# The first layer's memory values as seven half-size products, woven with two query heads

## The chip, the cores and the metric

The kernel runs on one core of a Trainium2 chip. The metric is device time in microseconds (us) of one execution, from the program's start to its end. TensorE (PE) multiplies matrices into PSUM banks of 128 partitions by 512 numbers; VectorE (DVE), ScalarE (ACT) and GpSimd (POOL) work on SBUF and PSUM; SyncE (SP) issues most transfers. Each engine runs its own instructions in order and waits on semaphores for those of others.

## The reference, cut to what matters

Two layers (512 positions, width 1024): each a mixer, a cross-attention into 256 memory rows and a SwiGLU feed-forward, all with a norm before and a norm after. The first layer's mixer is forgetting attention (FoX) beside a short gated convolution. All numbers are 32-bit floats.

```python
for layer in range(DEPTH):
    h = rmsnorm(x, g_mix_pre[layer])
    y = fox_shortconv_mixer(h, ...) if layer % 2 == 0 else rglru_mixer(h, ...)
    x = x + rmsnorm(y, g_mix_post[layer])
    h = rmsnorm(x, g_cross_pre[layer])
    m = rmsnorm(mem, g_mem[layer])
    y = memory_cross_attention(h, m, w_xq[layer], w_xkv[layer], w_xo[layer])
    x = x + rmsnorm(y, g_cross_post[layer])
    ...

def memory_cross_attention(h, m, w_q, w_kv, w_o):
    q = (h @ w_q).reshape(bsz, seq, MEM_HEADS, MEM_HEAD_DIM)
    k, v = jnp.split(m @ w_kv, 2, axis=-1)
    ...
```

The change concerns v of the first layer, a product of 256 x 1024 by 1024 x 1024, and the two first heads of q (512 x 1024 by 1024 x 256 each).

## The kernel before, in words

**Products.** A product of floats is made as three on TensorE: each operand is split into a rounded part hi and a rest lo, and hi·hi, hi·lo and lo·hi are added in one bank. `split_out` (L553-562) makes the two: a CAST on ScalarE (L556) and a subtraction on VectorE (L557). Weights come in pieces of 128 x 1024 numbers (512 KB) on SP's queue into one of four raw tiles `st`, and are split into one of four pairs `wh`, `wl` (`load_w`, L111-137).

**Stages around the change.** FoX ends with the output projection's second half (`half1`, L617-637). There each of four blocks of 128 positions of x is finished (`chain`, L638-650): the sum of squares on ScalarE (L221), a factor by small operations on VectorE (L225, L229) and a power on POOL (L233), x updated from two halves ya and yb (L642, L645). Then follow the next norm, two more sums of squares, a factor and the product h (L259). TensorE transposes h (L306) into a bank, and ScalarE and VectorE bring it out as hTh and hTl (`put_T`, L315 and L316). The blocks t = 0 and 1 are transposed between the matmuls of `half1`, t = 2 and 3 at the end of the keys. Between them the memory rows are transposed (L1034), copied out as `mTr` (L1037), stored to DRAM for the second layer as memT (L1050, POOL) and scaled by the gain g_mem and split into `mT` (L1043 ScalarE, L1044 VectorE).

**Keys, values, heads.** `memory_kv` (L1057-1093) computes the keys in four chunks of 256 columns with the banks of pool A (L1071, L1072; taken out by L1074, L1075 and split into kh, kl), then the transposes of blocks 2 and 3 into banks of pool B (`between`), then the values in two halves of 512 columns, also in pool A: for each of two halves 8 row blocks of weights x 2 blocks of memory rows x 3 matmuls (L1088-1090), taken out by four splits. `cross` then runs the query heads (`q_head`, by `ws_gemm` and `mm3`, L336-339): the weights stand still as lhsT and hT moves.

**Order.** The order of TensorE is the order in which the program is written. The order on the other engines is set by the tile scheduler from its own estimates. Two lists give the DRAM-side sums of the feed-forward's down projection, which is already made of seven products: `copies` are DRAM-to-DRAM copies, which `pace` issues on SP after three of every four weight loads; `adds` are transfers that add to DRAM, which `spend` issues on POOL, at some places behind a one-column copy `at` (L151) that waits for a given tile. `weave` runs two generators of matmul steps, a step of the one and a step of the other in turn.

Of the kernel before, what the change touches and what calls it, by code (L numbers as in the profile page):

```python
# [8 lines left out]
F32 = mybir.dt.float32  # L9
# [17 lines left out]
HOOKS = 0, 2  # L27
G = 14
SB = 8
GB = 6  # L30
# [12 lines left out]
def trunk_kernel(ctx: ExitStack, tc: tile.TileContext, a: dict, out: bass.AP):  # L43
# [625 lines left out]
    class DownProj(OutProj):  # L669
# [56 lines left out]
        def put_y(self, jp):  # L726
            if jp in self.stg:
                pool[0] = nc.gpsimd.dma_start(out=self.y[:, jp // 2, :, jp % 2, :],
                                              in_=self.stg[jp].rearrange("p m h c -> p (m h) c")).ins
                if jp:  # L730
                    spend(1)

# [266 lines left out]


    memT = dram.tile([P, KT, MEM], F32, name="memT")

# [16 lines left out]
    def memory_T(layer, bank):  # L1019
# [33 lines left out]
        if layer:  # L1053
            return vhl, (lambda: parts(range(4)), lambda: parts(range(4, KT)))
        return vhl, (lambda: turn(0), last)

    def memory_kv(layer, vhl, between):  # L1057

        w = a["w_xkv"][layer]
        kh_, kl_ = group("kh"), group("kl")  # L1060
        kh = kh_.rearrange("p a (b c) -> p (a b) c", c=MEM)
        kl = kl_.rearrange("p a (b c) -> p (a b) c", c=MEM)
        for c in range(4):
# [30 lines left out]

    def cross(layer, hT, kv, proj, hTf):
        kh, kl, vh, vl = kv
# [3 lines left out]
        qs, ps_, pts = {}, {}, {}  # L1100

        def q_head(h):
            banks = ws_gemm(wq, h * 256, hT)
            q = group("q")
            for m in range(2):
                split_out(banks[m], q[:, m, :], q[:, 2 + m, :], scale)
            qs[h] = q
            spend(3, f(q)[:, 3, 511:512])

# [50 lines left out]

        q_head(0)
        q_head(1)
        scores(0)
# [79 lines left out]
    def fox(proj):  # L1243
# [132 lines left out]
        TO = [(0, 0), (1, 0), (2, 0), (1, 384)]  # L1376

        def y_group(m):
            if m not in yg:
# [5 lines left out]
        def qk_pairs(m0):  # L1385
# [94 lines left out]
        def conv(m0):  # L1480
# [144 lines left out]

    hT = prev = None
    for layer in range(2):
# [3 lines left out]
        pf.plan()  # L1631
        pm = OutProj(a["ab_w_out"][0] if layer == 0 else a["c_w_out"][0], None, KT,
                     a["g_mix_post"][layer], a["g_cross_pre"][layer], hTc, *((bankA, bankB) if layer == 0 else (bankB, bankA)))
# [3 lines left out]
        else:  # L1637
            rglru(hT, prev, pm)
        vhl, steps = memory_T(layer, pm.first)
        pm.half1(steps)  # L1640
# [6 lines left out]

        kv = memory_kv(layer, vhl, rest)
        hTf = new_quads()
        pc = OutProj(a["w_xo"][layer], None, KT, a["g_cross_post"][layer], a["g_ffn_pre"][layer], hTf)  # L1650
        cross(layer, hTc, kv, pc, hTf)
        hT = new_hT() if layer == 0 else None
# [27 lines left out]
```

## Time and profile before

| | us |
|---|---|
| median of three runs | 1379.41 |
| lowest, highest | 1379.23, 1379.92 |
| the profiled execution | 1379.94 |
| its span, first to last instruction | 1378.2 |
| TensorE busy in it | 1368.9 |
| VectorE busy | 1119.8 |
| ScalarE busy | 730.9 |

The profile is one execution. A line such as L1088 is a line of the kernel before; matmuls overlap, so the time of one matmul is the distance between starts. The keys of the first layer begin at 227.1 us of the span, the transposes behind them at 249.7, the values at 251.4 and the first query head at 273.2.

### The profile page before, as it was taken

Reading aid. Unit: us, or ns where it says so; the run is one execution under the profiler, and the core shown is the slowest. Engines: PE = TensorE matmul, PEld = TensorE weight load, DVE = VectorE, ACT = ScalarE, POOL = GpSimd, SP = SyncE. Lnnn points to the kernel's source line nnn. Section 1 sums busy time; section 2 is a strip of 40 time slices with the busy share of each in tenths; the row PEclk is TensorE's granted clock in tenths of the full one; section 3 lists DMA queues with packets and bytes.
Section 4 is the critical chain, followed back from the end, with each engine's and each line's share of the span. In section 5 each row is a group of like instructions: output and inputs, shape, how many; then the busy total and the mean of one; then the engine's idle time right before and its main releaser. Section 6 shows DMA issues by size and latency. Waiting matters only on the chain.

```text
span 1378.2 us, 21545 instructions
## 1 busy us (share of the span) xinstructions
PE 1368.9 (99%) x8262; PEld 1217.7 (88%) x8262; DVE 1119.8 (81%) x1850; ACT 730.9 (53%) x1206; POOL 111.2 (8%) x160
## 2 busy tenths in 40 slices
PE   9999999999999999999999999999999999999998
PEld 7888788888899999998889888888889999999886
DVE  6777778635589999989898898764568999999987
ACT  5345466534464444456684896553456444445664
POOL 1000001012000101000011000101200011000001
PEclk9999999999999999999999999999999999999999
DMA  6854353668125557566666657357712555666654
GB/s 222 287 174 162 109 194 88 206 154 169 62 92 167 150 148 187 161 246 217 201 221 189 217 170 246 84 185 156 155 61 93 169 155 171 157 176 237 201 190 144
DMA packets 155107, 233.34 MB, mean 169 GB/s; under 512 B 8462, under 2 KB 90482, under 8 KB 153724
## 3 DMA queue, kind: packets, MB, share of 16 engines
q1 hardware_dynamic: 134420, 179.73, 39.5%
q0 software_dynamic: 17072, 46.16, 15.2%
q10 hardware_dynamic: 3512, 6.08, 1.4%
q8 instruction: 65, 1.06, 0.3%
q14 instruction: 38, 0.31, 0.1%
HBM read 219.34 MB, written 58.74 MB: 202 GB/s over the span
## 4 chain that ended last, share of the span: by engine, by line
PE 99%; DVE 0%; DMA 0%; ACT 0%; issue 0%; DVEq 0%; SPq 0%; ACTq 0%
PE bA L337 13%; PE bA L339 13%; PE bA L338 13%; PE bB L337 6%; PE bB L338 6%; PE bB L339 6%; PE bB L822 3%; PE bB L823 3%; PE bB L821 3%; PE bA L1071 2%; PE bA L822 2%; PE bA L823 2%; PE bA L821 2%; PE bA L580 2%; PE bA L582 2%; PE bB L582 2%
## 5 line engine op out<-in xcount | busy, mean ns | idle before, releaser
L557 DVE TENSOR_TENSOR wl<-st,wh 128x1024 fp32r<-128x1024 f32 x108 | 131.2, 1220 | 83.9 <-ACT wh L556 83.3
L556 ACT CAST wh<-st 128x1024 fp32r<-128x1024 f32 x108 | 113.1, 1050 | 107.9 <-PE bA L338 55.1
L337 PE MATMUL bA<-hTh,wh 128*128 128x512 f32 (+1 forms) x440 | 168.6, 383 | 0.0
L339 PE MATMUL bA<-hTh,wl 128*128 128x512 f32 (+1 forms) x440 | 165.6, 376 | 0.0
L338 PE MATMUL bA<-hTl,wh 128*128 128x512 f32 (+1 forms) x440 | 165.5, 376 | 0.0
L448 ACT CAST wg<-wr 128x1024 fp32r<-128x1024 f32 x80 | 83.6, 1046 | 48.9 <-DVE wr L477 38.5
L787 ACT CAST wh<-st 128x1024 fp32r<-128x1024 f32 x76 | 74.9, 985 | 62.4 <-PE bA L823 27.0
L449 DVE TENSOR_TENSOR wg<-wr,wg 128x1024 fp32r<-128x1024 f32 x80 | 97.1, 1214 | 0.0
L337 PEld LDWEIGHTS bA<-hTh,wh 128*128 128x128 f32 x440 | 82.9, 188 | 15.3 <-issue 1.0
L339 PEld LDWEIGHTS bA<-hTh,wl 128*128 128x128 f32 x440 | 82.8, 188 | 15.3
L338 PEld LDWEIGHTS bA<-hTl,wh 128*128 128x128 f32 x440 | 83.0, 189 | 13.8
L792 DVE TENSOR_TENSOR wl<-st,wh 128x1024 fp32r<-128x1024 f32 x76 | 86.1, 1133 | 10.2 <-ACT wh L787 10.1
L448 ACT CAST wh<-tt 128x1024 fp32r<-128x1024 f32 x40 | 42.1, 1053 | 61.4 <-DVE tt L477 61.4
L337 PE MATMUL bA<-hTq,wh 128*128 128x256 f32 x208 | 59.2, 284 | 0.0
L339 PE MATMUL bA<-hTq,wl 128*128 128x256 f32 x208 | 58.9, 283 | 0.0
L338 PE MATMUL bA<-hTq,wh 128*128 128x256 f32 x208 | 58.8, 283 | 0.0
L821 PE MATMUL bB<-wh,ya 128*128 128x512 f32 x148 | 57.6, 389 | 0.0
L822 PE MATMUL bB<-wl,ya 128*128 128x512 f32 x148 | 57.6, 389 | 0.0
L823 PE MATMUL bB<-wh,ya 128*128 128x512 f32 x148 | 57.6, 389 | 0.0
L767 DVE TENSOR_TENSOR ya<-yb,ya 128x512 fp32r<-128x512 f32 x84 | 53.3, 638 | 0.0
L821 PE MATMUL bA<-wh,ya 128*128 128x512 f32 x132 | 51.3, 389 | 0.0
L822 PE MATMUL bA<-wl,ya 128*128 128x512 f32 x132 | 51.3, 389 | 0.0
(385 smaller groups left out, 4396.9 us busy)
## 6 DMA issues: line engine op xcount, KB each, us to landing
wr<-in_w_ffn_gu_dram SPq DMA_DIRECT2D x80, 512.0 KB
st<-t SPq DMA_DIRECT2D x40, 512.0 KB
t<-in_w_ffn_down_dram SPq DMA_DIRECT2D x32, 512.0 KB
st<-in_w_xkv_dram SPq DMA_DIRECT2D x32, 512.0 KB
st<-in_w_ffn_down_dram SPq DMA_DIRECT2D x30, 512.0 KB
st<-in_ab_w_in_dram SPq DMA_DIRECT2D x24, 512.0 KB
y<-yr POOLq DMA_DIRECT2D x18, 512.0 KB, 4.7
t<-in_w_ffn_down_dram POOLq DMA_DIRECT2D x16, 512.0 KB, 8.7
```

Of the source, the lines that this page charges most:

```text
L337: nc.tensor.matmul(out=ps, lhsT=wh, rhs=xh, start=first, stop=False)
L338: nc.tensor.matmul(out=ps, lhsT=wh, rhs=xl, start=False, stop=False)
L339: nc.tensor.matmul(out=ps, lhsT=wl, rhs=xh, start=False, stop=last)
L448: return (lambda: nc.scalar.copy(out=to[0], in_=src), lambda: nc.vector.tensor_tensor(out=to[1], in0=src, in1=f(to[0]), op=ALU.subtract))
L449: lambda: nc.vector.tensor_tensor(out=to[1], in0=src, in1=f(to[0]), op=ALU.subtract))
L556: nc.scalar.copy(out=hi, in_=src)
L557: nc.vector.tensor_tensor(out=lo, in0=src, in1=f(hi), op=ALU.subtract)
L787: nc.scalar.copy(out=self.wt[s][0], in_=self.st[s])
L792: nc.vector.tensor_tensor(out=lo, in0=self.st[s], in1=f(hi), op=ALU.subtract)
L821: nc.tensor.matmul(out=banks[t], lhsT=yh, rhs=wh[:, jj, :], start=first and jj == 0, stop=False)
L822: nc.tensor.matmul(out=banks[t], lhsT=yh, rhs=wl[:, jj, :], start=False, stop=False)
L823: nc.tensor.matmul(out=banks[t], lhsT=yl, rhs=wh[:, jj, :], start=False, stop=last and jj == n - 1)
```

## The change

The values of the first layer become seven products of half size by Winograd's form of Strassen's scheme. With the normed memory split into row halves and inner halves (a11 ... a22) and the weights into inner and column halves (b11 ... b22), the seven products are a11·b11, s2·t2, n3·t3, a22·t4, n1·t1, a12·b21, n4·b22, each of 128 x 512 by 512 x 512.

- The weight sums t1 ... t4 are made in DRAM: eight copies of 512 KB on SP, ahead of the down projection's twenty in the list, and eight adding transfers on POOL, each behind an `at` copy, issued at the end of FoX's key groups and of the c, u and b groups of the convolution (`early`).
- The sums of the memory side are made in SBUF (`operands`): eight scalings of `mTr` in place (ScalarE, L1030 of the changed kernel), four subtractions (VectorE, L1033), four splits into tiles `va`.
- The 28 steps of three matmuls of the values (L1067-1069 of the changed kernel, banks of pool B) alternate with the 32 steps of query heads 0 and 1 (banks of pool A). The weights for the values are 14 loads of 512 KB instead of eight.
- The products are added by seven operations on VectorE and one copy on ScalarE, and split into the same vh and vl as before.
- The line in `put_y` issues the same number of adds per call as before for a list of this length.

The second layer's values are as before.

```diff
+SEVEN = (0,)
...
+    class Values:
+        ORDER = (("a11", "b11"), ("s2", "t2"), ("n3", "t3"), ("a22", "t4"), ("n1", "t1"), ("a12", "b21"), ("n4", "b22"))
...
+        def plan(self):
+            for k0 in (0, 2):
+                for to, frm, add in (("t3", "b12", "b22"), ("t2", "b11", "t3"), ("t4", "b21", "t2"), ("t1", "b11", "b12")):
+                    copies.append(lambda to=to, frm=frm, k0=k0: nc.sync.dma_start(
+                        out=self.rows(to, k0), in_=self.rows(frm, k0)))
+                    adds.append(lambda to=to, add=add, k0=k0: nc.gpsimd.dma_start(
+                        out=self.rows(to, k0), in_=self.rows(add, k0), accum_op=ALU.add))
+        def operands(self, raw, vhl, layer):
+            for k in range(KT):
+                nc.scalar.mul(out=raw[:, k, :], in_=raw[:, k, :], mul=ch("gm", 8 * layer + k))
+            e, l = slice(0, P), slice(P, MEM)
+            a21, a11, a22, a12 = raw[:, 0:4, e], raw[:, 0:4, l], raw[:, 4:8, e], raw[:, 4:8, l]
+            sub = lambda o, i0, i1: nc.vector.tensor_tensor(out=o, in0=i0, in1=i1, op=ALU.subtract)
+            sub(a21, a21, a11)
+            sub(a22, a22, a21)
+            sub(a11, a11, a22)
+            sub(a12, a12, a22)
+            gs = [group("va") for _ in range(2)]
...
+                split_out(src, hi, lo)
...
+        def steps(self):
...
+            def put(j, nh, ps, other, op):
+                tt(other, ps, other, op)
+                split_out(other, vh[:, 2 * j + nh, :], vl[:, 2 * j + nh, :])
...
+            for a_, b_ in self.ORDER:
+                ps = bankB()
+                for k0 in (0, 2):
+                    st = wst.tile([P, 2, 512], F32, tag="st", name="st")
+                    pace(nc.sync.dma_start(out=st, in_=self.rows(b_, k0)))
+                    wh, wl = split_w(st, 2, 512)
+                    for kk in range(2):
+                        k = k0 + kk
+                        hi, lo = self.parts[a_][k]
+                        nc.tensor.matmul(out=ps, lhsT=hi, rhs=wh[:, kk, :], start=k == 0, stop=False)
+                        nc.tensor.matmul(out=ps, lhsT=hi, rhs=wl[:, kk, :], start=False, stop=False)
+                        nc.tensor.matmul(out=ps, lhsT=lo, rhs=wh[:, kk, :], start=False, stop=k == 3)
+                        yield 1
+                if b_ == "b11":
+                    nc.scalar.copy(out=p1, in_=ps)
+                elif b_ == "t2":
+                    tt(q, ps, p1, ALU.subtract)
...
         between()
+        if values:
+            values.operands(raw, vhl, layer)
+            return kh, kl, None, None
...
-        q_head(0)
-        q_head(1)
+        if values:
+            weave(values.steps(), q_steps(0, 1))
+            vh, vl = values.out
+        else:
+            q_head(0)
+            q_head(1)
         scores(0)
...
+        owed = [8 if 0 in SEVEN else 0]
+        def early(ap):
+            if owed[0]:
+                owed[0] -= 1
+                spend(1, ap)
...
+                early(f(qk[m0 + 1])[:, 3, 511:512])
...
+                early(cs[m0 + 1][:, 511:512])
...
+                early(cs[m0 + 1][:, 511:512])
...
+                early(f(yg[m0 + 1])[:, 3, 511:512])
...
+    if 0 in values:
+        values[0].plan()
```

Lines of the changed kernel stand one to about a hundred further on than the same lines before (L221 is L222, L259 is L260, L315 is L316, L1037 is L1125). The order of instructions moves at these places.

ScalarE, from the memory's scaling (L1043, now L1131) to the evictions of the transposes of block 1 of x (`x_112` is that block; `post` and `pre` are the factors of the norms behind and ahead). Before:

```order
L1043 ACTIVATE mT<-mTr,chan 128x256 x8
L315 CAST hTh<-bA 128x4x128 x2
L221 ACTIVATE junk,pre<-x_112 128x512 x2
L221 ACTIVATE junk,post<-bB 128x512
L315 CAST hTh<-bA 128x4x128 x2
L221 ACTIVATE junk,pre<-x_113 128x512 x2
```

The change:

```order
L1131 ACTIVATE mT<-mTr,chan 128x256 x8
L316 CAST hTh<-bA 128x4x128 x2
L222 ACTIVATE junk,pre<-x_112 128x512
L1030 ACTIVATE mTr<-mTr,chan 128x256
L222 ACTIVATE junk,pre<-x_112 128x512
L1030 ACTIVATE mTr<-mTr,chan 128x256
L222 ACTIVATE junk,post<-bB 128x512
L1030 ACTIVATE mTr<-mTr,chan 128x256 x6
L316 CAST hTh<-bA 128x4x128 x2
```

All eight scalings now stand ahead of the second pair of casts. VectorE in the same stretch, before:

```order
L1044 SCALAR_TENSOR_TENSOR mT<-mTr,chan,mT 128x256 x8
L316 TENSOR_TENSOR hTl<-bA,hTh 128x4x128 x2
L225 TENSOR_SCALAR pre<-pre 128x1
L229 SCALAR_TENSOR_TENSOR pre<-pre 128x1
L259 SCALAR_TENSOR_TENSOR h<-x_112,pre,gain 128x512 x2
L229 SCALAR_TENSOR_TENSOR post<-post 128x1
L642 TENSOR_TENSOR yb<-bB,gain 128x512
```

The change:

```order
L1132 SCALAR_TENSOR_TENSOR mT<-mTr,chan,mT 128x256 x8
L317 TENSOR_TENSOR hTl<-bA,hTh 128x4x128
L230 SCALAR_TENSOR_TENSOR post<-post 128x1
L646 SCALAR_TENSOR_TENSOR x_113<-ya,post,x_113 128x512
L317 TENSOR_TENSOR hTl<-bA,hTh 128x4x128
L226 TENSOR_SCALAR pre<-pre 128x1
L1033 TENSOR_TENSOR mTr<-mTr 128x4x128
L230 SCALAR_TENSOR_TENSOR pre<-pre 128x1
L1033 TENSOR_TENSOR mTr<-mTr 128x4x128
L260 SCALAR_TENSOR_TENSOR h<-x_112,pre,gain 128x512 x2
```

Two subtractions, the factor `post` and one update of block 2 now stand ahead of h of block 1.

TensorE at the end of the keys (L1071 and L1072, now L1160 and L1161; `wh` ahead of `mT` are weights that move against memory rows that stand, in the values). Before:

```order
L1072 MATMUL bA<-mT,wl 128x256
L306 MATMUL bB<-ident,h 128x128 x16
L1088 MATMUL bA<-wh,mT 128x512
L1089 MATMUL bA<-wl,mT 128x512
L1090 MATMUL bA<-wh,mT 128x512
L1088 MATMUL bA<-wh,mT 128x512
```

The change:

```order
L1161 MATMUL bA<-mT,wl 128x256
L307 MATMUL bB<-ident,h 128x128 x16
L1067 MATMUL bB<-wh,mT 128x512
L1068 MATMUL bB<-wl,mT 128x512
L1069 MATMUL bB<-wh,mT 128x512
L338 MATMUL bA<-hTh,wh 128x512
L339 MATMUL bA<-hTl,wh 128x512
L340 MATMUL bA<-hTh,wl 128x512
```

The values now write banks of the pool that the transposes used, and a query step, which reads hT, comes after the first three matmuls.

POOL in FoX, from the transfer of the cumulative gates (`cum`) and the first loads of `cb` to the last memset (`vt` are the weight sums in DRAM). Before:

```order
L1371 DMA cum<-e 8x512
L1407 DMA cb<-cum 128x512 x2
L1493 MEMSET cu 128x2 x2
L1407 DMA cb<-cum 128x512 x6
L1493 MEMSET cu 128x2 x2
```

The change:

```order
L1517 DMA cb<-cum 128x512 x2
L152 COPY at<-qk 128x1
L1024 DMA vt_0_123<-in_w_xkv_dram 128x2x512
L152 COPY at<-cs 128x1
L1024 DMA vt_0_122<-vt_0_123 128x2x512
L1604 MEMSET cu 128x2 x2
L152 COPY at<-cs 128x1
L1024 DMA vt_0_124<-vt_0_122 128x2x512
L1517 DMA cb<-cum 128x512 x2
L152 COPY at<-y 128x1
L1024 DMA vt_0_121<-in_w_xkv_dram 128x2x512
L1517 DMA cb<-cum 128x512 x2
```

Two adding transfers stand ahead of the memsets, and four ahead of the fifth load of `cb`.

More of the change, by code (lines that the diff above doesn't have):

```diff
@@ L730, in put_y @@
                 if jp:
-                    spend(1)
+                    spend(-(-len(adds) // (self.NJ - 2 - jp)))
         def load_y(self, i):
@@ L998, in mid, with __init__, rows @@
                 put_T(self.hT, 3, self.hs[3], halves=(0,))
+    class Values:
+        ORDER = (("a11", "b11"), ("s2", "t2"), ("n3", "t3"), ("a22", "t4"), ("n1", "t1"), ("a12", "b21"), ("n4", "b22"))
+        RAW = {"b11": (0, 0), "b12": (0, 1), "b21": (1, 0), "b22": (1, 1)}
+        def __init__(self, layer):
+            self.w = a["w_xkv"][layer]
+            self.sums = {n: dram.tile([4 * P, 512], F32, name=f"v{n}_{layer}") for n in ("t1", "t2", "t3", "t4")}
+        def rows(self, name, k0):
+            if name in self.RAW:
+                r, c = self.RAW[name]
+                v = self.w[r * 512:r * 512 + 512, D + c * 512:D + c * 512 + 512]
+            else:
+                v = self.sums[name]
+            return v.rearrange("(k p) n -> p k n", p=P)[:, k0:k0 + 2, :]
+        def plan(self):
[16 more added lines that the diff above has]
+            gs = [group("va") for _ in range(2)]
+            self.parts = {}
+            for n, (name, src) in enumerate((("s2", a22), ("n3", a21), ("n1", a11), ("n4", a12))):
+                g = gs[n // 2]
+                hi, lo = (g[:, n % 2 * 2 + i, :].rearrange("p (k c) -> p k c", c=P) for i in range(2))
+                split_out(src, hi, lo)
+                self.parts[name] = [(hi[:, k, :], lo[:, k, :]) for k in range(4)]
+            for name, k0, c in (("a11", 0, P), ("a22", 4, 0), ("a12", 4, P)):
+                self.parts[name] = [(vhl[k][:, c:c + P], vhl[k][:, MEM + c:MEM + c + P]) for k in range(k0, k0 + 4)]
+        def steps(self):
+            self.out = vh, vl = group("vh"), group("vl")
+            tt = lambda o, i0, i1, op: nc.vector.tensor_tensor(out=o, in0=i0, in1=i1, op=op)
+            def put(j, nh, ps, other, op):
+                tt(other, ps, other, op)
+                split_out(other, vh[:, 2 * j + nh, :], vl[:, 2 * j + nh, :])
+            p1, q, v, c = (sbuf(n) for n in ("vp", "vq", "vv", "vc"))
+            for a_, b_ in self.ORDER:
[15 more added lines that the diff above has]
+                    tt(q, ps, p1, ALU.subtract)
+                elif b_ == "t3":
+                    tt(v, ps, q, ALU.add)
+                elif b_ == "t4":
+                    tt(c, ps, v, ALU.subtract)
+                    split_out(c, vh[:, 0, :], vl[:, 0, :])
+                elif b_ == "t1":
+                    put(0, 1, ps, v, ALU.add)
+                    tt(q, ps, q, ALU.add)
+                elif b_ == "b21":
+                    put(1, 0, ps, p1, ALU.add)
+                else:
+                    put(1, 1, ps, q, ALU.add)
@@ L1053, in memory_T, with memory_kv @@
         if layer:
-            return vhl, (lambda: parts(range(4)), lambda: parts(range(4, KT)))
-        return vhl, (lambda: turn(0), last)
-    def memory_kv(layer, vhl, between):
+            return (raw, vhl), (lambda: parts(range(4)), lambda: parts(range(4, KT)))
+        return (raw, vhl), (lambda: turn(0), last)
+    def memory_kv(layer, mem, between, values):
+        raw, vhl = mem
         w = a["w_xkv"][layer]
@@ L1093, in memory_kv, with cross @@
         return kh, kl, vh, vl
-    def cross(layer, hT, kv, proj, hTf):
+    def cross(layer, hT, kv, proj, hTf, values):
         kh, kl, vh, vl = kv
@@ L1100, in cross, with q_steps, put @@
         qs, ps_, pts = {}, {}, {}
-        def q_head(h):
[L1103 to L1108, printed above, removed]
+        def q_steps(*hs):
+            for h in hs:
+                def put(banks, h=h):
+                    q = group("q")
+                    for m in range(2):
+                        split_out(banks[m], q[:, m, :], q[:, 2 + m, :], scale)
+                    qs[h] = q
+                    spend(3, f(q)[:, 3, 511:512])
+                yield from ws_steps(wq, h * 256, hT, put)
+        def q_head(h):
+            for _ in q_steps(h):
+                pass
         def scores(h):
@@ L1159, in av @@
                 o.hi[2 * h + m], o.lo[2 * h + m] = og[:, m, :], og[:, 2 + m, :]
-        q_head(0)
-        q_head(1)
+        if values:
+            weave(values.steps(), q_steps(0, 1))
+            vh, vl = values.out
+        else:
+            q_head(0)
+            q_head(1)
         scores(0)
@@ L1626, in trunk_kernel @@
     hT = prev = None
+    values = {layer: Values(layer) for layer in SEVEN}
+    if 0 in values:
+        values[0].plan()
     for layer in range(2):
@@ L1631, in trunk_kernel @@
         pf.plan()
+        if layer == 0 and 1 in values:
+            values[1].plan()
         pm = OutProj(a["ab_w_out"][0] if layer == 0 else a["c_w_out"][0], None, KT,
@@ L1638, in trunk_kernel @@
             rglru(hT, prev, pm)
-        vhl, steps = memory_T(layer, pm.first)
+        mem, steps = memory_T(layer, pm.first)
         pm.half1(steps)
@@ L1646, in rest @@
                 pm.transpose(t)
-        kv = memory_kv(layer, vhl, rest)
+        kv = memory_kv(layer, mem, rest, values.get(layer))
         hTf = new_quads()
         pc = OutProj(a["w_xo"][layer], None, KT, a["g_cross_post"][layer], a["g_ffn_pre"][layer], hTf)
-        cross(layer, hTc, kv, pc, hTf)
+        cross(layer, hTc, kv, pc, hTf, values.get(layer))
         hT = new_hT() if layer == 0 else None
```

## The prediction

> **What bounds the kernel now.** The page's busy line comes first, then its chain of waits, then TensorE's list of waits (columns: engine, tile, line, what it waited for, us in total, times, longest).
>
> ```profile
> PE 1368.9 (99%) x8262; PEld 1217.7 (88%) x8262; DVE 1119.8 (81%) x1850; ACT 730.9 (53%) x1206; POOL 111.2 (8%) x160
> ...
> PE 99%; DVE 0%; DMA 0%; ACT 0%; issue 0%; DVEq 0%; SPq 0%; ACTq 0%
> ...
> PE bA L1257 <- POOL ident masks.py:199: 1.5, 1, 1.5
> PE bB L1425 <- DVE yt L1474: 0.3, 1, 0.3
> PE bA L1270 <- ACT hTh L315: 0.3, 1, 0.3
> ```
>
> TensorE sets the end everywhere; its waits sum to 2.1 us. Fewer matmuls therefore shorten the kernel one for one, and a new wait of TensorE lengthens it one for one; no old wait is left to be won back. The stages of layer 0 that the change touches, each row from start to end, with us, then PE, PEld, DVE, ACT and POOL busy with their counts, granted clock, DMA share and GB/s:
>
> ```profile
> 205.00:228.00 23.00, 23.00 (x120) 19.39 (x119) 17.80 (x42) 15.51 (x41) 5.00 (x9) 1.00 0.21 77
> 228.00:250.00 22.00, 22.00 (x127) 19.14 (x126) 16.95 (x27) 12.45 (x23) 2.30 (x3) 1.00 0.64 174
> 251.70:290.00 38.30, 38.30 (x171) 31.70 (x170) 20.08 (x23) 16.17 (x21) 1.34 (x2) 1.00 0.53 166
> 290.00:309.00 19.00, 19.00 (x98) 16.20 (x97) 8.42 (x14) 6.52 (x15) 3.59 (x4) 1.00 0.88 186
> ```
>
> The first is the second half of the output projection with the norms and transposes of x, the second the keys, the third the values and the first query heads. VectorE is 77% busy in the first two (17.80 of 23, 16.95 of 22) and 52% in the third.
>
> **What is saved.** The values have 2 x 8 x 2 x 3 = 96 matmuls of 512 columns; seven products of 4 x 3 make 84. What one is worth is read from starts, not from its duration:
>
> ```profile
> 249.68 1.91 PE L306 MATMUL bB<-ident,h 128*128 128x128 f32 x16
> 251.35 0.48 PE L1088 MATMUL bA<-wh,mT 128*128 128x512 f32 x1
> ...
> 252.12 0.39 PE L1088 MATMUL bA<-wh,mT 128*128 128x512 f32 x1
> ...
> 273.20 0.39 PE L337 MATMUL bA<-hTh,wh 128*128 128x512 f32 x1
> ...
> L1088 PE MATMUL bA<-wh,mT x64: 389/389/476, 251.3 to 924.1; 128*128 128x512 f32 x64
> ```
>
> The fourth of the values' matmuls starts at 252.12 and the first query matmul behind all 96 at 273.20: 93 starts in 21.08 us, 0.227 each, though each lasts 0.39: they overlap. So 12 matmuls fewer are **-2.72 us** (12 x 0.227), not the 4.7 that 12 x 0.389 would make. A step of three is 0.68 us.
>
> **Place A: the operands, in front of a norm that TensorE needs.** The order of the change puts the eight scalings (L1030) and the first two of four subtractions (L1033) on ScalarE and VectorE between the sum of squares of x's second row block and the h that TensorE transposes. Before, this stretch was (start, us, engine, line):
>
> ```profile
> 215.28 3.31 ACT L1043 ACTIVATE mT<-mTr,chan 128x256 fp32r<-128x256 f32 x8
> 218.48 1.05 ACT L315 CAST hTh<-bA 128x512 fp32r<-128x512 f32 x2
> 219.43 0.64 ACT L221 ACTIVATE junk<-x 128x512 bf16<-128x512 f32 x1
> ...
> 220.99 0.60 ACT L221 ACTIVATE junk<-bB 128x512 bf16<-128x512 f32 x1
> 221.48 0.20 ACT L221 ACTIVATION_READ_ACCUMULATOR junk<-bB 128x1 f32 x1
> ...
> 221.24 0.16 DVE L229 SCALAR_TENSOR_TENSOR pre<-pre 128x1 f32<-128x1 f32 x1
> 222.09 1.41 DVE L259 SCALAR_TENSOR_TENSOR h<-x,pre,gain 128x512 f32<-128x512 f32 x2 [0.69 <-POOL pre L233]
> 223.49 0.68 DVE L642 TENSOR_TENSOR yb<-bB,gain 128x512 f32<-128x512 f32 x1
> 224.23 0.75 DVE L645 SCALAR_TENSOR_TENSOR x<-ya,post,x 128x512 f32<-128x512 f32 x1
> ...
> 215.69 0.59 POOL L1050 DMA_DIRECT2D memT<-mTr  x1 [0.44 <-ACT mTr L1037]
> ...
> memT<-mTr POOLq DMA_DIRECT2D x1, 1024.0 KB, 4.2
> ...
> 223.46 1.03 PE L306 MATMUL bA<-ident,h 128*128 128x128 f32 x8
> ```
>
> The first half of h is done at 222.8 (222.09 + 0.70) and TensorE takes it at 223.46: 0.65 us of slack. Now with the new order. A scaling writes the tile that the transfer of memT still reads, so the first cannot start before that lands at 219.9 (215.69 + 4.2). One is like an L1043, 0.41 us (3.31 / 8). ScalarE: first half of the sum of squares to 220.15, a scaling to 220.6, second half (0.7) to 221.3, a scaling to 221.75, the sum of squares over bB (0.7) to 222.5, six scalings to 225.0. VectorE, in order: the small factor of `post` at 222.5, 0.8 until POOL's power is back (221.24 to 222.09 above is 0.85), x from ya 0.75 to 224.1, an hTl of 0.64 (1.28 / 2, quoted under place B), a 0.15 op to 225.0, L1033 (like the 0.68 of L642) to 225.7, the factor `pre` to 225.85, the second L1033, which waits for all scalings, to 226.55 while POOL's power runs to 226.7, then the first half of h to 227.4 and the second to 228.1. TensorE, which meets these transposes in its written order with the last matmuls of the projection and all of K behind, stands from 223.46 to 227.4. **+3.95 us.** Low end 3.3: if subtractions take 0.64 and scalings 0.36 (a copy of 128x256, ks in the next fence but this one) and the second half adds nothing. High end 6: the memT transfer lands 2 us later, since transfers for the weight sums now run near it (a small cb load lands between 3.4 and 6.5 us there, row under place D). Zero is excluded unless these engines do not run in the order given.
>
> [...]
>
> **K phase.** Two subtractions before it, and four splits of 0.66 on ScalarE and 0.69 on VectorE (like kh and kl below) inside it, raise VectorE to 16.95 + 2.8 = 19.7 of 22 us and ScalarE to 15.1: covered by K's own matmuls, with about 1 us to spare at the tightest split. If that cover went, 0.7 us a split. Taken as 0; 0 to +1.4.
>
> **Place B: end of K.** What ran before on ScalarE and VectorE while V's matmuls already went (TensorE at 251.35):
>
> ```profile
> 250.77 0.36 ACT L1074 COPY ks<-bA 128x256 f32<-128x256 f32 x1
> 251.03 2.05 ACT L315 CAST hTh<-bB 128x512 fp32r<-128x512 f32 x4
> 252.94 0.66 ACT L556 CAST kh<-ks 128x512 fp32r<-128x512 f32 x1
> ...
> 252.38 1.28 DVE L316 TENSOR_TENSOR hTl<-bB,hTh 128x512 fp32r<-128x512 f32 x2
> 253.63 0.69 DVE L557 TENSOR_TENSOR kl<-ks,kh 128x512 fp32r<-128x512 f32 x1
> 254.23 1.28 DVE L316 TENSOR_TENSOR hTl<-bB,hTh 128x512 fp32r<-128x512 f32 x2
> ```
>
> V before used bank A and needed no hT; its 21.8 us covered these transposes' evictions wholly. Now the first V step writes a bank B that still holds a transpose until its hTl is taken: 252.38 + 0.65 = 253.05, against 251.35: +1.7. It then has one step of 0.68 (to 253.75), and the second matmul of the first query step, due at 253.97, reads the third hTl, which stands behind kl and is done at 254.23 + 0.68 = 254.9: +0.95. Sum **+2.7 us** on top of a K that ends later by place A. Low end 1.7 (the second stall is taken up, if VectorE does kl while TensorE stands); high end 3.7 if VectorE, fuller in K, comes 1 us late.
>
> **Place C: the weave.** 84 + 96 matmuls take 40.9 us. In them 18 weight loads are split (14 for V, 4 for two heads):
>
> ```profile
> L557 DVE TENSOR_TENSOR wl<-st,wh 128x1024 fp32r<-128x1024 f32 x108 | 131.2, 1220 | 83.9 <-ACT wh L556 83.3
> L556 ACT CAST wh<-st 128x1024 fp32r<-128x1024 f32 x108 | 113.1, 1050 | 107.9 <-PE bA L338 55.1
> ```
>
> VectorE: 18 x 1.22, and 15 operations of about 0.69 (seven sums, four splits, four of q): 32.3 of 40.9 us. ScalarE: 18 x 1.05 and some nine of 0.66: 25. Both fit, but not at each point: the two heads hold two of the four split buffers, V turns over the other two, and one is freed every four steps, 2.72 us, while its next content needs 1.05 + 1.22 = 2.27. Where the split of the fourth product (0.66, 0.69) and the first head's four evictions stand ahead, once, the walk through the order gives a stall of **+0.75 us**. Low end 0, high end 3 (each load late by one eviction).
>
> **Place D and the rest.** The eight additions go to POOL's queue among FoX's loads of cb, each behind a small copy that waits for a tile of ScalarE or VectorE:
>
> ```profile
> 87.04 0.71 POOL L1407 DMA_DIRECT2D cb<-cum  x1 [4.97 <-DVE cs L1500]
> ...
> 100.95 0.29 DVE L1433 TENSOR_TENSOR cb<-cb,mask 128x128 f32<-128x128 f32 x1
> ...
> DMA to landing us min/median/max: 3.4/3.7/6.5
> ```
>
> Behind the waiting copies stand only later cb loads and a memset. The load issued at 87.04 is used at 100.95, 14 us on, and lands 3.7 after issue: 10 us of slack, and the tiles the copies name are written within that time by the order. Taken as 0, to +0.5; with that distance gone a late cb would stop VectorE, and TensorE behind it, for its 3.7 us. On SP the eight copies go ahead of the down projection's twenty, which move later by eight places, still within K's loads; their sums are read only in the FFN. Layer 1 keeps its values; 0.
>
> **Sum**: -2.72 + 3.95 + 2.7 + 0.75 = +4.7 on the profiled execution's 1379.94, that is 1384.6; that execution is 0.53 above the median of 1379.41, so **1384.1 us**, 0.34% slower.
>
> **Rivals.** *The saving wins* (chance 0.07): ScalarE and VectorE hide both A and B. It asks that the h of the second block be ready within the 0.65 us of slack and that the transposes' evictions end 1.7 us earlier; then 1379.41 - 2.72 = 1376.7, faster. For it: both engines are idle over a fifth of these stages. Against: it is order, not load, that delays h. It decides from a sum of stalls under 2.7 us. *One stall only* (0.17): either A holds and B is filled by VectorE's work done while TensorE stood (-2.72 + 3.95 = +1.2, 1380.6), or B and C hold and A shrinks to 1 (-2.72 + 2.7 + 0.75 + 1 = +1.7, 1381.1): within 0.2%. *Transfers starve the weave* (0.10): 18 loads of 0.524 MB less a lead of four in buffers are 7.3 MB; at the 166 GB/s of the third window 44.2 us instead of 40.9: +3.3, 1387.4. For it: the fourth window shows DMA at 88% with only 186 GB/s. Against: the raw tiles give a lead of up to eight. *Slow after the stall* (0.06): the trace has one start after idleness and one in full run:
>
> ```profile
> 1.47 3.03 PE L1257 MATMUL bA<-ident 128*128 128x128 f32 x13 [1.47 <-POOL ident masks.py:199]
> ...
> 207.15 1.04 PE L1034 MATMUL bA<-ident,mem 128*128 128x128 f32 x8
> 207.95 0.48 PE L580 MATMUL bB<-rh,y 128*128 128x512 f32 x1
> ```
>
> 13 in 3.03 is 0.23 each, against 0.10 (0.80 / 8): half the rate or less for 3 us. After place A such a phase would cost about 1.7 us (13 x 0.13), 1385.8. [...]
>
> **How the numbers follow.** The forecast case has 0.60, from 1382 to 1386.5 by its own bounds. Faster holds the first rival, 0.07; same (within 0.2%, 2.76 us, about what a measurement of this kernel can tell from no change) the second and a little of the forecast's low end, 0.20; the rest, 0.73, is slower. The range leaves out the first rival, and a tenth in all at the two ends of the others: 1379.8 to 1388.
>
> **What would show it.** Right: TensorE's list of waits has L307 behind DVE h at about 4 us, L1067 behind DVE hTl near 1.7, L339 behind hTl near 1, and the V stretch has 84 matmuls with starts 0.23 apart. Wrong: the h row at about 222 as before, V starting right behind the transposes, or waits at L1067 of a microsecond and more at many steps.

## The result and the profile after

The changed kernel took 1386.8 us (median of 6 runs, 1386.3 to 1389.49) against 1379.56 (6 runs, 1379.23 to 1380.16): 7.2 us or 0.53% slower, ratio 1.0053 with a 95% interval of 1.0042 to 1.0063. Its profiled execution took 1387.29 us, with a span of 1384.6, 6.4 more than before; the rest lies outside the span, on which more below. A few single executions, of the kernel before too, took 1.4 to 3.2 times as long; the medians and ratios below leave them out.

The page's busy line and chain, and TensorE's waits between 200 and 340 us, of the changed kernel:

```profile
PE 1369.1 (99%) x8250; PEld 1216.4 (88%) x8250; DVE 1135.5 (82%) x1871; ACT 742.5 (54%) x1225; POOL 124.8 (9%) x176
...
PE 97%; DVE 1%; ACT 1%; DMA 0%; POOL 0%; issue 0%; DVEq 0%; SPq 0%; ACTq 0%
...
PE bA L307 <- DVE h L260: 3.6, 1, 3.6
PE bB L1067 <- DVE hTl L317: 1.5, 1, 1.5
PE bA L339 <- DVE hTl L317: 0.7, 1, 0.7
PE bB L1068 <- DVE wl L558: 0.5, 1, 0.5
```

Twelve matmuls are gone (8250), and four waits are new. The first is at the transposes of block 1 of x, the second and third at the start of the weave, the fourth inside it. Busy time of TensorE has not fallen with the matmuls, 1369.1 against 1368.9. Where that went is seen in its rows behind the first wait, and in the stages cut at them (granted clock third from the end):

```profile
223.03 0.39 PE L583 MATMUL bB<-rh,y 128*128 128x512 f32 x1
226.98 1.67 PE L307 MATMUL bA<-ident,h 128*128 128x128 f32 x8 [3.56 <-DVE h L260]
228.30 0.77 PE L581 MATMUL bB<-rh,y 128*128 128x512 f32 x1
...
229.72 0.63 PE L581 MATMUL bB<-rh,y 128*128 128x512 f32 x1
230.15 0.63 PE L582 MATMUL bB<-rl,y 128*128 128x512 f32 x1
...
232.46 0.39 PE L1160 MATMUL bA<-mT,wh 128*128 128x512 f32 x1
...
228.00:230.00 2.00, 2.00 (x8) 1.71 (x7) 1.83 (x4) 1.51 (x5) 0.00 (x0) 0.50 0.03 8
226.98:232.46 5.48, 5.45 (x20) 4.40 (x21) 4.87 (x10) 2.52 (x6) 0.93 (x1) 0.69 0.01 3
232.46:255.07 22.61, 22.61 (x129) 19.60 (x128) 18.49 (x31) 15.02 (x27) 2.23 (x3) 1.00 0.58 161
258.49:301.19 42.70, 41.51 (x180) 33.74 (x181) 29.66 (x33) 21.51 (x25) 4.47 (x4) 1.00 0.70 209
```

Behind the wait of 3.56 us matmuls follow each other by 0.43 (229.72 to 230.15) where 0.23 was usual, and the granted clock is 0.69 over that stretch and 0.50 from 228 to 230. This is called the slow phase below. The keys take 22.61 us as before. The keys began at 227.08 before and at 232.46 now; up to the last matmul before the transposes the changed kernel was 0.19 earlier (223.03 against 223.22), so place A cost 5.57. Step by step, each from the starts of TensorE in the two traces:

| | us |
|---|---|
| start of the transposes of block 1, 223.46 to 226.98, with the 0.19 | +3.7 |
| their second half, waiting for the second half of h | +0.3 |
| slow phase behind them | +1.6 |
| end of keys to the first step of the values, 1.67 to 3.42 | +1.75 |
| weave: 42.70 against 43.61 before | -0.9 |
| sum | +6.4 |

The last row but one is the saving of 2.72, less 0.84 at the first query step and 1.0 of waits for split weights and small gaps. On VectorE place A looks like this:

```profile
221.99 0.16 DVE L230 SCALAR_TENSOR_TENSOR post<-post 128x1 f32<-128x1 f32 x1 [1.71 <-ACT junk L222]
222.83 0.75 DVE L646 SCALAR_TENSOR_TENSOR x<-ya,post,x 128x512 f32<-128x512 f32 x1 [0.68 <-POOL post L234]
223.50 0.68 DVE L317 TENSOR_TENSOR hTl<-bA,hTh 128x512 fp32r<-128x512 f32 x1
224.16 0.68 DVE L1033 TENSOR_TENSOR mTr<-mTr 128x512 f32<-128x512 f32 x1
224.95 0.69 DVE L1033 TENSOR_TENSOR mTr<-mTr 128x512 f32<-128x512 f32 x1
226.08 1.41 DVE L260 SCALAR_TENSOR_TENSOR h<-x,pre,gain 128x512 f32<-128x512 f32 x2 [0.44 <-POOL pre L234]
```

These are the rows that the prediction had worked out, about half a microsecond earlier than it had them. Read alone they say that scalings and subtractions made h late. The runs say otherwise for the larger part.

### The profile page after: what moved, and what is told of

It reads as the page before. It is cut to its first block, busy times and chain, and to the rows that moved or that the text cites. A ratio compares the mean times of both kernels' runs of the same rounds, so it can differ in the third digit from the quotient of the medians.

```text
span 1384.6 us, 21617 instructions
## 1 busy us (share of the span) xinstructions
PE 1369.1 (99%) x8250; PEld 1216.4 (88%) x8250; DVE 1135.5 (82%) x1871; ACT 742.5 (54%) x1225; POOL 124.8 (9%) x176
## 4 chain that ended last, share of the span: by engine, by line
PE 97%; DVE 1%; ACT 1%; DMA 0%; POOL 0%; issue 0%; DVEq 0%; SPq 0%; ACTq 0%
PE bA L338 13%; PE bA L340 13%; PE bA L339 13%; PE bB L338 6%; PE bB L339 6%; PE bB L340 6%; PE bB L822 3%; PE bB L824 3%; PE bB L823 3%; PE bA L1160 2%; PE bA L822 2%; PE bA L824 2%; PE bA L823 2%; PE bA L581 2%; PE bA L583 2%; PE bA L582 2%
## 5 line engine op out<-in xcount | busy, mean ns | idle before, releaser
L558 DVE TENSOR_TENSOR wl<-st,wh 128x1024 fp32r<-128x1024 f32 x114 | 138.6, 1220 | 75.0 <-ACT wh L557 74.4
L557 ACT CAST wh<-st 128x1024 fp32r<-128x1024 f32 x114 | 119.5, 1051 | 110.8 <-PE bA L339 45.9
L788 ACT CAST wh<-st 128x1024 fp32r<-128x1024 f32 x76 | 74.9, 985 | 63.0 <-PE bA L824 27.0
L793 DVE TENSOR_TENSOR wl<-st,wh 128x1024 fp32r<-128x1024 f32 x76 | 86.1, 1133 | 10.2 <-ACT wh L788 10.2
L234 POOL TENSOR_TENSOR post<-post,nhalf 128x1 f32<-128x1 f32 x23 | 14.3, 621 | 433.2 <-DVE post L230 419.5
```

The lines of the kernel that those rows point to most:

```text
L557: nc.scalar.copy(out=hi, in_=src)
L558: nc.vector.tensor_tensor(out=lo, in0=src, in1=f(hi), op=ALU.subtract)
L788: nc.scalar.copy(out=self.wt[s][0], in_=self.st[s])
L793: nc.vector.tensor_tensor(out=lo, in0=self.st[s], in1=f(hi), op=ALU.subtract)
```

## The experiments

Theory 1 was that of the prediction: ScalarE and VectorE have the operands' work in front of h, TensorE stands, and (seen only in the result) it runs slow for a while behind a stall of 3.56 us. Theory 2 put the loss on the transfers for the weight sums. Theory 3, that only the scalings cost, stands in the first expectation; theory 4 came out of the runs. Each ratio is to the kernel before on the same chip, whose median was 1379.48 us beside the first four runs, 1379.56 beside the three with rows or transposes moved, 1379.50 beside the first run of the buffer and the three behind it, and 1379.71 beside the second run of the buffer.

### The scalings later

```diff
-            for k in range(KT):
-                nc.scalar.mul(out=raw[:, k, :], in_=raw[:, k, :], mul=ch("gm", 8 * layer + k))
+            for k in range(KT):
+                with tc.issue_after(gates[k // 4]):
+                    nc.scalar.mul(out=raw[:, k, :], in_=raw[:, k, :], mul=ch("gm", 8 * layer + k))
```

`gates` are copies of ks on ScalarE in the first and second chunk of the keys. By theory 1 the factor `post` of block 2, its update from ya and an hTl still stand ahead of h on VectorE: that is the first sum below.

> The changed kernel, with the eight scalings of the operands queued on ScalarE behind evictions of the first and second chunk of the keys. [...] Factor at 221.5, update 222.35 to 223.1, hTl to 223.75, the two small factors and POOL to 224.85, first half of h at 225.55, TensorE ready at 223.27: a stall of 2.3 us in place of 3.56, and no slow phase behind it (2.0). 1386.8 - 1.3 - 2.0 = 1383.5 us. Theory 2 (the transfers for the weight sums are what costs): 1386.8. Theory 3 (only the scalings cost, and the order without them is that of before): 1386.8 - 5.6 = 1381.2.

1383.3 us (1382.87 to 1386.05), ratio 1.0029 (1.0018 to 1.0041). On TensorE, VectorE and in the stage behind the wait:

```profile
225.55 1.29 PE L307 MATMUL bA<-ident,h 128*128 128x128 f32 x8 [2.32 <-DVE h L260]
...
223.04 0.69 DVE L317 TENSOR_TENSOR hTl<-bA,hTh 128x512 fp32r<-128x512 f32 x1
...
226.00:228.00 2.00, 1.97 (x12) 1.61 (x11) 1.83 (x4) 1.71 (x4) 0.00 (x0) 1.00 0.03 8
```

A wait of 2.32 is left, though no scaling and no subtraction stands there any more. So their work explains 1.24 of 3.56, and something else the rest; theory 3 falls. That no slow phase stands behind a stall of 2.3 us was the author's estimate: the clock stays at 1.00 in this execution, but it falls to 0.50 behind a wait of 2.32 with the buffer by itself, below.

### Useless matmuls in the stall

```diff
+            for _ in range(0 if hf else warm):
+                nc.tensor.transpose(out=ps[:, 0:P], in_=ident, identity=ident)
```

with `warm` = 30 for block 1 of the first layer, else 0.

> The changed kernel, with 30 transposes of the identity by TensorE into the bank that the first transposes of block 1 then overwrite: about 3.0 us of work of no use, put into the stall of 3.56. The wait for h stays. Theory 1 (idleness of TensorE brings the slow phase): the matmuls behind the transposes are 0.23 apart instead of 0.43, granted clock 1.00 there instead of 0.60, and the time falls by the slow phase's 2.0 us to 1384.8. Rival (the slow phase has another cause, or the stall's end moves with the added work): 1386.8 or up to 3 more.

1384.49 us (1384.08 to 1384.98), ratio 1.0036 (1.0023 to 1.0048). TensorE's rows and the stage behind them:

```profile
222.60 3.33 PE L307 MATMUL bA<-ident 128*128 128x128 f32 x29
226.11 1.38 PE L309 MATMUL bA<-ident,h 128*128 128x128 f32 x8 [0.18 <-DVE h L260]
...
226.50:231.00 4.50, 4.40 (x24) 3.58 (x23) 4.01 (x9) 3.17 (x8) 0.41 (x1) 1.00 0.00 0
```

h comes as late as before against the matmuls ahead of it, and the time falls by 2.3 us, 1.9 of them in the median span (1384.5 to 1382.6): with TensorE kept busy, but for a wait of 0.18 us, the clock reads 1.00 from 226.5 to 231, where the changed kernel has 0.64. In these two kernels the slow phase came with the idleness and went with it.

### The memory-side sums alone, and the weight sums alone

The first has scalings, subtractions and splits in the kernel before, their results not used; the second has only the eight copies and eight adding transfers, their results not used. In both the values are computed as before.

```diff
         if values:
             values.operands(raw, vhl, layer)
-            return kh, kl, None, None
```

> The kernel before with the memory-side sums alone (eight scalings, four subtractions, four splits, their results not used), without the weight sums, the products and the weave. Theory 1: place A has the whole loss, 3.56 of stall and 2.0 of slow phase, and nothing else changes: 1379.6 + 5.6 = 1385.2 us. Theory 2 (transfers): 1379.6.

> The kernel before with the weight sums alone: eight copies on SP and eight adding transfers with their small copies on POOL, results not used, values as before. Theory 1: nothing waits for them, 1379.6 within 0.5 us. Theory 2 (the transfers delay loads or POOL's work): 1381 to 1384, with new waits of TensorE in FoX or in the keys.

The memory-side sums alone: 1384.71 us (1383.97 to 1385.69), ratio 1.0037 (1.0024 to 1.0049); 5.2 us more than the kernel before, nearly all of place A. The weight sums alone: 1380.24 (1379.71 to 1381.61), ratio 1.0006 (0.9997 to 1.0015), no difference that can be told. Theory 2 falls. In the profiled execution of the first the same wait is there, and the clock behind it is not lowered:

```profile
226.53 1.29 PE L307 MATMUL bA<-ident,h 128*128 128x128 f32 x8 [3.56 <-DVE h L260]
...
226.00:228.00 2.00, 1.43 (x10) 1.21 (x11) 1.83 (x4) 0.73 (x2) 0.00 (x0) 1.00 0.00 0
228.00:230.00 2.00, 2.00 (x11) 1.61 (x10) 2.00 (x5) 1.79 (x5) 0.00 (x0) 1.00 0.04 8
```

That execution took 1383.97 with a mean clock of 0.999; the other four took 1384.52 to 1385.69 at 0.997 to 0.998. So one wait of one length seems to have a slow phase behind it in some executions and not in others; the four were not profiled.

### The old order of rows as well

The kernel with late scalings, and besides the small factor of a block on VectorE queued behind h of the block before:

```diff
-    def rstd(st):
+    def rstd(st, behind=None):
...
+        with tc.issue_after(behind) if behind else nullcontext():
+            nc.vector.scalar_tensor_tensor(
+                out=st[:, 3:4], in0=st[:, 1:2], scalar=1.0 / D, in1=st[:, 2:3],
+                op0=ALU.mult, op1=ALU.add,
+            )
...
-            r = rstd(st)
+            r = rstd(st, last_h[0] if t and self.rowed else None)
```

> The kernel with late scalings, and besides the small factor of a block on VectorE queued behind h of the block before, so that the order of that stretch is again that of the kernel before. Theory 1 (the whole of place A is order): no wait at the transposes of block 1, keys from 227.1 us; against late scalings alone 2.3 us less: 1383.3 - 2.3 = 1381.0 us. Rival (the late update and hTl that h was charged with are forced by something else, such as POOL's queue): 1383.3. With all four subtractions and four splits inside the keys VectorE has some 22.5 us of work in 22.6: up to +1 us of new waits there.

1385.28 us (1384.66 to 1385.86), ratio 1.0041 (1.0028 to 1.0053): no gain, but 2 us more than with late scalings alone. The expectation failed. The 2 us are near what the slow phase cost in the changed kernel (1.6), and this profile has one (last row), that of late scalings none. The row on VectorE that shows why the wait is still there is the second:

```profile
219.68 0.69 DVE L320 TENSOR_TENSOR hTl<-bA,hTh 128x512 fp32r<-128x512 f32 x1
223.39 0.69 DVE L320 TENSOR_TENSOR hTl<-bA,hTh 128x512 fp32r<-128x512 f32 x1 [3.02 <-PE bB L587]
...
225.99 1.75 PE L310 MATMUL bA<-ident,h 128*128 128x128 f32 x8 [2.48 <-DVE h L263]
...
228.00:230.00 2.00, 2.00 (x6) 1.61 (x5) 1.91 (x4) 1.71 (x5) 0.00 (x0) 0.50 0.00 0
```

The second hTl of block 0, which in the kernel before ran straight behind the first at 220.4, waits 3.02 us for a matmul of the projection. L587 is the matmul with `rl`, the rests of the projection's last weights. Large tiles come from a pool of 14 places, and a new tile takes over the place of an old one. In the built program of the kernel before that hTl has the address of mTr, and its waits name mTr's last readers (the transfer of memT and L1044). In the changed kernel mTr is still needed for the operands; the hTl has the address of that `rl`, and its waits name the last matmul with it. Theory 4 followed: place A is mostly a buffer held longer, and the order of VectorE in which `post` and an update stood ahead of h was the scheduler's answer to an hTl that could not run.

### Transposes earlier

The transposes of blocks 2 and 3 in front of the last chunk of the keys, once on top of the kernel just shown, once on the changed kernel alone:

```diff
             s = sbuf("ks")
+            if c == 3 and values:
+                between()
             for m in range(2):
...
-        between()
+        if not values:
+            between()
```

> As the kernel with late scalings and the old order of rows, and the transposes of blocks 2 and 3 moved ahead of the last chunk of the keys, 5.7 us earlier. Theory 1 (place B is the distance between transposes and weave): no wait for hTl at the first step of the values or of the queries; 2.2 to 2.6 us less than without this move: 1381.0 - 2.4 = 1378.6 us, 0.9 under the kernel before. What is left of the saving of 2.72 is the wait for split weights in the weave (0.5 and some small ones) and VectorE's fuller keys. Rival (the split weights of the weave come late as well, hidden behind the wait for hTl): the wait moves to the first weights, 1380 or more.

> The changed kernel with only the transposes of blocks 2 and 3 moved ahead of the last chunk of the keys; place A untouched. Theory 1: places A and B add up; B's 2.4 us go, A's 3.56 and the slow phase stay: 1386.8 - 2.4 = 1384.4 us. Rival (with place A the h of block 3 or the eviction comes too late for the earlier place): 1386 to 1387, with a wait for h at the moved transposes.

On top of late scalings and the old order: 1384.14 us (1382.73 to 1384.49), ratio 1.0030 (1.0019 to 1.0041). On the changed kernel alone: 1383.73 (1383.12 to 1384.02), ratio 1.0028 (1.0017 to 1.0038), 3.1 less than without. The first had been expected at 1378.6 on a base of 1381.0; its base came out at 1385.28, and of the 2.4 us the move brought 1.1. TensorE's waits of the first, then of the second:

```profile
PE bA L310 <- DVE h L263: 2.5, 1, 2.5
PE bB L1074 <- DVE wl L561: 1.9, 3, 1.1
```

```profile
PE bA L307 <- DVE h L260: 3.5, 1, 3.5
...
PE bB L1068 <- DVE wl L558: 0.5, 1, 0.5
PE bB L307 <- DVE h L260: 0.5, 1, 0.5
```

In both the waits for hTl at the start of the weave are gone, as expected: place B is the distance between transposes and weave. In the first, waits for split weights (1.9) took their place: there the rival was right. That all sums and splits had been put into the keys is the likely reason; in the profile without the move, that of the old order of rows, VectorE is busy without a break from 238.9 to 260.5 us. In the second a wait of 0.5 for h at the moved transposes is new.

### The buffer by itself

The kernel before, with one instruction more, which reads mTr again. In the program it stands behind the keys; the scheduler let it run inside them, at 234.01 us, 15 us behind the other readers of mTr, which are done at 219.2. Two runs; the profile is that of the second:

```diff
         between()
+        if not layer:
+            nc.scalar.copy(out=stats("kp")[:, 0:1], in_=keep[0][:, 0, 0:1])
```

> The kernel before, with one more instruction in the first layer: behind the keys ScalarE copies one number per partition out of mTr, the tile of the transposed memory. So that tile is held until then, as in the changed kernel; none of the new work is done. Theory 4 (a buffer, not the work): of the pool of 14 large tiles the second hTl of block 0 took over mTr's in the kernel before; now it must take the tile of the projection's last weight rests, which TensorE reads until about 223; VectorE, in order, has h of block 1 behind it. Wait for h at the transposes of block 1 of 2.3 to 2.5 us, keys later by as much, 1379.5 + 2.4 = 1381.9 us, and up to 2 more in executions with a slow phase. Theory 1 as first put (scalings and subtractions in front of h are what makes it late): 1379.5, no wait.

> The kernel before with mTr held until behind the keys, once more for an undisturbed profile: the first one's whole execution was slowed to 4403 us. Theory 4: the trace shows the second hTl of block 0 waiting on VectorE for TensorE's last matmul with the projection's weight rests (start at 223.0 to 223.5 instead of 220.4), TensorE waiting 2.3 to 2.5 us for h of block 1, and 1381.9 us if the granted clock stays at 1.00 behind that wait, 1383.9 if it falls. Rival (the longer time comes from the added copy behind the keys): wait there, none at h.

First: 1383.84 us (1381.87 to 1383.97), ratio 1.0029 (1.0017 to 1.0041). Second: 1382.86 (1382.18 to 1383.85), ratio 1.0022 (1.0012 to 1.0032). The waits of TensorE, its last matmul with `rl`, VectorE's rows, the added copy and a stage, of the second:

```profile
PE bA L306 <- DVE h L259: 2.3, 1, 2.3
...
222.35 0.39 PE L581 MATMUL bB<-rl,y 128*128 128x512 f32 x1
...
222.78 0.69 DVE L316 TENSOR_TENSOR hTl<-bA,hTh 128x512 fp32r<-128x512 f32 x1
224.38 1.42 DVE L259 SCALAR_TENSOR_TENSOR h<-x,pre,gain 128x512 f32<-128x512 f32 x2 [0.66 <-POOL pre L233]
...
234.01 0.18 ACT L1082 COPY kp<-mTr 128x1 f32<-128x1 f32 x1
...
228.00:230.00 2.00, 2.00 (x6) 1.54 (x6) 1.15 (x4) 0.72 (x2) 0.55 (x1) 0.50 0.00 0
```

One copy of 128 numbers, itself 9 us behind the wait, makes h of block 1 late by the same 2.3 us that were left when the scalings had gone: it keeps the hTl from mTr's place. No wait appears at the copy, so the rival falls. The ten runs of the second form two groups: five of 1382.18 to 1382.34, and five of 1383.37 to 1383.85; the profiled one belongs to the second and has a clock of 0.50 from 228 to 230. Without a slow phase the buffer costs 2.6 us, with one 4. The wait is shown, and that it is this tile too: in the built program the hTl now has the address of `rl` and waits for the last matmul with it, and in the trace it starts at 222.78, when that matmul is done (222.35 + 0.39). It had been expected at 223.0 to 223.5; the whole stretch runs a little earlier. An update of block 2 and the factor `post` have moved ahead of the hTl here as well, with none of the new work in the kernel.

### The tile given up, and the memory loaded again

```diff
+            if c == 0 and values:
+                raw = f(group("mTr")).rearrange("p a (b c) -> p (a b) c", c=MEM)
+                nc.scalar.dma_start(out=raw, in_=memT)
```

> The changed kernel, with mTr given up as in the kernel before and the memory loaded again from DRAM for the scalings (1 MB, issued on ScalarE's queue once the projection's tile is free; it lands in the keys). Theory 4: no wait at the transposes of block 1 and no slow phase, though nothing was done about the order; places B and C stay: 1386.8 - 5.6 = 1381.2 us. Theory 1 as first put (the order of the scalings): also about 1381.2, since they move too; but against late scalings with the old order of rows (1385.3, wait 2.5) the two differ only in the buffer. Rival (something else delays h): 1383 to 1385.

1381.93 us (1380.67 to 1383.76), ratio 1.0019 (1.0010 to 1.0029): 4.9 us less than the changed kernel. TensorE at block 1, at the first query step, and a stage behind that:

```profile
222.85 1.03 PE L307 MATMUL bA<-ident,h 128*128 128x128 f32 x8
...
252.90 0.50 PE L1067 MATMUL bB<-wh,mT 128*128 128x512 f32 x1 [1.25 <-DVE hTl L317]
...
255.03 0.50 PE L339 MATMUL bA<-hTl,wh 128*128 128x512 f32 x1 [0.94 <-DVE hTl L317]
...
256.00:258.00 2.00, 2.00 (x6) 1.59 (x5) 0.71 (x1) 0.84 (x1) 0.00 (x0) 0.50 0.14 26
```

The transposes of block 1 start straight behind the matmuls, with no rule on the order at all, and in the built program the hTl has mTr's address again. That is what theory 4 says. By itself this run does not decide, since the scalings moved with the reload; the buffer by itself does. The 0.7 above the expected 1381.2 is explained by the last row: in this execution, of 1382.98 us, a slow phase came behind place B, after waits of 1.25 and 0.94. The five runs with a mean clock of 0.999 took 1380.67 to 1381.72, the five with 0.998 took 1382.14 to 1383.76.

### All of it together

The kernel that loads the memory again, with the earlier transposes, and two of the four splits (n1, n4) moved into the weave:

```diff
+            part(0, "s2", a22)
+            part(1, "n3", a21)
+            self.later = {"t2": lambda: part(2, "n1", a11), "t3": lambda: part(3, "n4", a12)}
...
+                if b_ in self.later:
+                    self.later[b_]()
```

> As the one that loads the memory again, with the transposes of blocks 2 and 3 ahead of the last chunk of the keys, and the splits of two of the four sums (n1, n4) moved behind the second and third product of the weave. Theory 4 and place B as measured: no waits for h or hTl; 1381.2 - 2.4 = 1378.8 us, with 0.5 to 1 us of waits for split weights left in the weave. Rival (VectorE, now with about 24 us of work in the 22.6 of the keys, becomes the bound at the end of the keys): 1380 to 1381, waits for wl at the first steps of the weave.

1379.24 us (1377.86 to 1380.18), ratio to the kernel before 0.9997 (0.9988 to 1.0006): 7.6 us less than the changed kernel, and no difference from the kernel before. TensorE's new waits:

```profile
PE bA L1171 <- DVE ks L1175: 0.7, 1, 0.7
PE bB L1072 <- DVE wl L558: 0.5, 1, 0.5
```

Of the 2.72 saved, 1.2 goes into these two waits, at the first chunk of the keys and in the weave. The median span is 0.7 shorter than that of the kernel before (1377.0 against 1377.7), but 2.1 to 3.3 us lie outside the span, against 1.7 to 1.9; where the rest went is not shown. VectorE was taken to be the engine that bounds what is left. The next run took work from it:

```diff
-            sub = lambda o, i0, i1: nc.vector.tensor_tensor(out=o, in0=i0, in1=i1, op=ALU.subtract)
+            sub = lambda o, i0, i1: nc.gpsimd.tensor_tensor(out=o, in0=i0, in1=i1, op=ALU.subtract)
```

> As the one before, with the four subtractions on POOL instead of VectorE: VectorE has 2.8 us less in the keys. If VectorE is what is left (rival there): 0.5 to 1.5 us less than without, 1377.5 to 1378.5. If not: no difference. If POOL's subtractions are long (over 2 us each) or slow VectorE beside them: 1379 or more.

1383.61 us (1383.06 to 1385.57), ratio 1.0033 (1.0021 to 1.0046), 4.4 more. POOL, VectorE and TensorE in the keys:

```profile
237.78 5.03 POOL L1033 TENSOR_TENSOR mTr<-mTr 128x512 f32<-128x512 f32 x3
...
237.06 4.62 DVE L260 SCALAR_TENSOR_TENSOR h<-x,pre,gain 128x512 f32<-128x512 f32 x2 [0.73 <-POOL pre L234]
...
242.16 0.47 PE L1171 MATMUL bA<-mT,wh 128*128 128x512 f32 x1 [3.53 <-DVE ks L1175]
...
244.00:246.00 2.00, 2.00 (x9) 1.71 (x7) 2.00 (x4) 1.78 (x4) 0.00 (x0) 0.50 0.42 107
```

The two halves of h, 1.41 with the subtractions on VectorE, take 4.62 beside POOL's three subtractions, ks comes late behind them, and TensorE stands for 3.53, with a slow phase behind it (last row). An update of x (L646) beside POOL's first subtraction, 1.48 from 231.91, takes 1.79 in place of 0.75. So VectorE was slowed in this stage while POOL worked; by what, no run shows. The third case of the expectation came true, and whether VectorE is what is left stays open.

## Why the prediction was right or wrong

The direction and the mechanism in its outline held, and 1386.8 lies inside the range, above the likeliest value of 1384.1. By steps:

- **The saving of 2.72** was there: 84 matmuls at 0.227, and the weave shorter by 0.9 in spite of its waits.
- **Place A, +3.95.** The size was near, 3.56 in the list of waits, but the cause was given wrongly, and the near size is no proof of it: the order that was summed already held the consequences of the late tile. The step that failed is the first sentence of that part, that the scalings and subtractions stand between and make h late. It took the order of VectorE as given and summed it; it did not ask why `post` and the update of block 2 had moved ahead of an hTl that ran at 220.4 before. The answer was in the waits of that hTl. By the runs, 2.3 us of the wait come from mTr being held longer, so that the hTl waits for the last matmul with `rl`, and 1.2 from the work.
- **The slow phase** had a chance of 0.06 at a price of 1.7. It came in the profiled execution, at 1.6, and probably in all six runs of the changed kernel: without it a span of 1383.0 would be expected, and the six have 1383.8 to 1386.2. The price was right; the chance was the author's estimate and far too low: of eight profiled executions with a wait of 2.3 to 3.6 us five had such a phase, two of them behind waits of 2.32 and 2.48. This term, left out of the sum, is the largest part of the miss.
- **K phase, 0**: 22.61 against 22.60 us, with VectorE at 18.49 where 19.7 were expected.
- **Place B, +2.7**: 1.75 and 0.84, as worked out. Earlier transposes took 3.1 away.
- **Place C, +0.75**: one wait of 0.5 at the place forecast, about 1.0 with the small ones.
- **Place D, 0**: the weight sums alone cost 0.7, with an interval that holds zero.
- The rival of a saving that wins fell with places A and B; that of starved transfers too, since no wait for a transfer appears and the weave moved 209 GB/s.

From -2.72 + 3.95 + 2.7 + 0.75 = 4.7, the measured steps are -2.72 + 4.0 + 1.6 + 1.75 + 0.84 + 1.0 = 6.5, against 6.4 in the span. The rest, about 0.7 in the medians, stays open: the six runs have 2.1 to 3.3 us outside their spans, runs of the kernel before 1.7 to 1.9. Some of the experiments have the larger share as well and others not, the useless matmuls (1.9) for one; no run tells what it is.

## What to carry to other kernels

Ask of each instruction that moved what it waits for in either program: an order that looks odd may be the scheduler's way round a tile that is no longer free. A tile that lives longer can be a cost by itself (2.6 us here), because the tile that would have taken its place must wait for another; loading the data again from DRAM was cheaper here, 1381.93 against 1386.8 us. A stall of TensorE had a second price behind it in some of these executions: of eight profiled ones with a wait of 2.3 to 3.6 us, five had a slow phase, which cost 1.6 us in the changed kernel.

## What the runs showed of the hardware

Behind a stall TensorE ran in some executions at a granted clock of 0.50, with matmuls 0.43 apart in place of 0.23 in the changed kernel. It did so after waits of 3.56 (the changed kernel), 3.54 (transposes earlier), 3.53 (subtractions on POOL), 2.48 (old order of rows) and 2.32 us (the buffer by itself), and after 1.25 and 0.94 within 3 us (the memory loaded again). It did not after 3.56 (memory-side sums alone), 2.5 (old order and earlier transposes) and 2.32 (late scalings), nor after the changed kernel's own 1.51 and 0.68 at the start of the weave. The clock did not fall in the stall, where the windows read 1.00, but after TensorE had started again, 0.1 us later with the transposes earlier and 1.6 us later with the buffer by itself. In five of the six profiles that have it the windows of 2 us give the phase one length, 3.4 us at 0.50: 0.93, 0.50 and 0.71 from 226 in the changed kernel, 0.65 and 0.50 from 226 with the old order of rows, 0.60 and 0.55 from 226 with the transposes earlier, 0.71, 0.50 and 0.93 from 226 with the buffer by itself, 0.90, 0.50 and 0.75 from 254 with the memory loaded again. In the sixth, with the subtractions on POOL, the clock reads 0.50 from 244 to 246, and pairs of matmuls start 0.64 apart, in place of 0.35, from 243.44 to 246.00. In ten runs of one kernel with one wait of 2.3 us there were two groups, 1.4 us apart. With the stall filled by useless transposes the profile shows 1.00, and all five runs have a mean clock of 0.999. Which waits have such a phase behind them, and why it is absent in other executions, no run shows.
